# A two-layer hybrid trunk on one core: elementwise chains moved into PSUM, and the mixer's norms, scan outcome and projection order rewritten

## The chip, the core and the metric

The kernel runs on one core of one Trainium2 chip, as one launch. The metric is device time in microseconds (us), the median of several executions. Beside it stands one execution that the hardware profiler recorded; all rows of the profile and of the trace come from that one.

A core has five engines with queues of their own, each of which works through its instructions in a fixed order: PE multiplies matrices (its weight loads, PEld, are shown apart), DVE, ACT and POOL work on elements, and SP issues DMAs. PE writes its results into PSUM, of which the kernel uses eight banks of 128 x 512 fp32. The other data lie in SBUF.

## The reference

Input is x, 512 positions of width 1024, in fp32. Sixteen learned meta tokens are put ahead, so the trunk runs over 528 positions. DEPTH is 2:

```
layer 0:  h += even_mixer(h);              h += mlp(h)
layer 1:  h += conformer_conv_module(h);   h += mlp(h)

even_mixer: u = rms_norm(h); q, k, v, z, xBC, dt = u @ w_in
    q, k: RMS norm per head (8 query heads, 2 key heads, 64 wide)
    att = attention over a window of 128 plus the meta tokens, with ALiBi and sinks
    xBC = silu(causal conv of 4 taps)
    y = state-space scan in chunks of 128 (16 heads, 2 groups, state of 64) + x * d_skip
    y = rms_norm per group of (y * silu(z))
    out = concat(att, y) @ w_out                    (1536 -> 1024)
conformer: u = rms_norm(h) @ pw1 (1024 -> 2048) + b; u = u[:1024] * sigmoid(u[1024:])
    u = causal depthwise conv, 31 taps; u = silu(layer_norm(u)); out = u @ pw2 + b
mlp: square(relu(rms_norm(h) @ w_up)) @ w_down      (1024 -> 4096 -> 1024)
```

The sixteen meta positions are dropped from the output.

## The kernel before

**Layout and precision.** Activations lie with the 1024 features as eight tiles of 128 partitions and the positions along the columns. The positions are cut into two streams: A (stream 0) has 272 columns, the 16 meta tokens and 256 positions, or 256 where the meta tokens are no longer needed; B (stream 1) has 256. Every dense product is made from two halves of each operand: a high part rounded to the matmul's fp32r type and a low part, the rest. A product of weights w and inputs x is hi(w)·hi(x) + hi(w)·lo(x) + lo(w)·hi(x), so each tile of 128 x 128 weights costs three matmuls. In the names, wh and wl are the parts of the weights, xh and xl, nh and nl, ah and al, oh and ol those of inputs. An output tile of 128 features with 8 input tiles takes 24 matmuls; eight such tiles, one half (up or down) of a quarter of the MLP for one stream, take 192.

**Weights.** SP loads them in pieces of 128x512 (pool wm) and, from out-projection 1 on, also 128x1024 (wp). ACT makes the high part (wh), and DVE or POOL the low part (wl = wr − wh).

**Who sets the order.** The program is written as generators ("threads": the main stream of products, the loader, the splitters, one for each tile's eviction, one for each norm and so on) that yield single operations with an estimated duration. A list scheduler (class Sched, lines 66 to 227) takes in each step, among the threads' next operations, the one that it believes can start first, by priority where starts are equal, and emits it to its engine; where an operation may go to DVE or to POOL it takes the one that it believes ends first. A number added to one of these ways is the `bias` for wl: with 0 the two are equal, with 3000 POOL is preferred. So each engine's order is fixed before the program runs, and it is the order of the scheduler's beliefs. All operations are recorded at the lines of the small helpers: L253 (two tensors, DVE) and L255 (POOL), L260 (scalar and two tensors, DVE), L267 (tensor and scalars, DVE), L275 (activation, ACT), L279 (copy or cast, ACT), L282 (copy, DVE), L288 (DMA), L307 (matmul), L314 (transpose on PE), L520 (reciprocal, DVE). For this reason the rows are told apart by the names of tiles.

**PSUM.** The eight banks are three of the kind "mm" (outputs of the dense products), three "bg" (norms, the scan, statistics) and two "at" (attention, convolution sums). Function pmm takes an "mm" bank and may borrow up to `wide` banks of "bg"; wide is 2 from out-projection 1 on.

**The stages** (function main), with the MLP's names: up, the layer, the quarter, the stream.

1. In-projection, 24 tiles for both streams (names in), in the order B, C, k, v, four of q, eight of x, eight of z (W_B to W_Z). Beside it run the threads of the norm, dt, the convolution of 4 taps, q/k norm (th_qk_norm), attention (att_a scores, att_b transposes of probabilities, att_c values), the scan (ssd_a to ssd_h) and its gated norm (ssd_norm: sn_a, sn_b).
2. Out-projection of stream A (out), which starts when the gated norm of A (norm0) is done, then two quarters of the MLP of A (up00A, dn00A, up01A, dn01A), beside which the mixer of B ends; out-projection of B; the other two quarters of A.
3. pw1 of A (pw), then the whole MLP 0 of B (up00B to dn03B); beside it DVE makes the depthwise convolution of A (th_conv, 31 taps of 256 columns for each of eight tiles, summed in two "at" banks; names conv, and Y for the last tap) and its layer norm (th_ln: names lna, lnm, ln, stln).
4. pw1 of B and pw2 of A (both pw), then the MLP 1 of A (up10A to dn13A), with the convolution and the layer norm of B beside it.
5. pw2 of B and the MLP 1 of B (up10B to dn13B), at whose end the outputs are stored.

**The chains that evict a tile.** For an up tile (ev_up in mlp): ut (SBUF) = max(psum, 0) · rb on DVE, and the bank is dropped; uq = square(ut) on ACT; ah = round(uq) on ACT; al = uq − ah on DVE or POOL. rb is the row norm's factor, spread over the partitions, so the norm is applied behind the product. For a tile that becomes the next norm's input (out-projection, the last dn quarter, pw2): h = psum + h on DVE, the bank is dropped, and then function prep makes nh = h · g (ACT), nl = h · g − nh (DVE), the square sqh (ACT) and acc += sqh (DVE) from h in SBUF. When all eight are there, row_norm sums acc over the partitions with a matmul by ones (st...), makes 1/sqrt by a root (ACT), a reciprocal and a Newton step of small DVE operations (rs_v, rs_t, rs_r), spreads it with a second matmul and copies it to rb (ACT). For pw1 (ev in pw1): ut = psum · rb, the bank is dropped; sg = sigmoid(ut + b) for one of two tiles, U = (ut + b) · sg for the other. The layer norm adds eight Y tiles on DVE (lna), takes their mean by a matmul, copies it to lnm, centres Y, squares and adds (lna), spreads the factor to rb, multiplies (Y), and makes silu and the two parts from SBUF.

Of the kernel before, what the change touches and what calls it, by code (L numbers as in the profile page):

```python
# [65 lines left out]
class Sched:  # L66
# [110 lines left out]
    def step(self):  # L177
# [27 lines left out]
        for th in self.threads:  # L205
# [5 lines left out]
            if op.table and op.table != self.table and op.ways[0][0] == "A":  # L211
                t += 1283
            p = th[1]
            key = (t, p() if callable(p) else p, th[4])
# [15 lines left out]
def trunk(ctx: ExitStack, tc: tile.TileContext, h0, vecs, cmat, selm, selmt, atab, atab0, w_in, w_dt, w_out,  # L230
# [127 lines left out]
    cm = const.tile([128, 520], F32, name="cm")  # L358
    ident, mle, mgt, ones = cm[:, 0:128], cm[:, 128:256], cm[:, 256:384], cm[:, 384:512]
    heads = cm[:, 512:520]  # L360
# [11 lines left out]
    bias = [0.0]  # L372
# [144 lines left out]
    def rsqrt(r, t, v):  # L517

        yield ACT(t, v, AF.Sqrt)
        yield VEC(1.04 * cols(r) + 150, lambda: nc.vector.reciprocal(r, t), r, t)  # L520
# [8 lines left out]
    def row_norm(s, a, blocks, eps, key):  # L529
# [6 lines left out]
                   for i, c in enumerate(blocks)))  # L536
# [8 lines left out]
                    ident[0:blk(c)[1], 0:blk(c)[1]], True, True) for i, c in enumerate(blocks)))  # L545
        yield CP(rb[s][:, :n], p[:, :n])
# [20 lines left out]
    def sumsq(a, x, first, begun, pool=False):  # L567
# [5 lines left out]
        else:  # L573
            q = yield take(tmp, [128, 272], F32, "sqh", 3)
# [3 lines left out]
            drop(q)  # L578
# [167 lines left out]
    conv4 = set()  # L746

    def th_silu():
# [9 lines left out]
        for s in range(2):  # L758
            yield lambda: conv4 >= set(range(W_Z, W_Z + 8))
            for k in range(0, 8, 4):  # L760
                x = sz[s][:, k:k + 4, :STREAM[s][1]]
                yield ACT(x, x, AF.Silu)
            done.add(f"z{s}")
# [28 lines left out]
    selr = m1.tile([10, 5, 128], F32R, name="selr")  # L792
    seltr = m1.tile([128, 5, 10], F32R, name="seltr")

    def th_qk_norm():

        yield after("sel")
        p = []
        for s in range(2):
            p.append((yield bank("bg", "qk_a")))  # L800
        for i in range(5):
            yield lambda: (W_K if i == 0 else W_Q + i - 1) in conv4
            x = kf if i == 0 else qf[:, i - 1]
# [41 lines left out]
        drop(a, b)  # L845
# [795 lines left out]
```

## Time and profile before

| | us |
| --- | --- |
| median of 3 runs | 1308.71 (1303.02 to 1311.38) |
| the profiled execution's own time | 1308.62 |
| its span, from first to last instruction | 1306.5 |
| PE busy in the span | 1241.0 (95%) |
| DVE busy | 960.0 (73%) |
| ACT busy | 679.4 (52%) |
| POOL busy | 487.8 (37%) |

The mean clock that was granted to PE is 0.969 of full speed. 2.1 us of the execution lie outside the span.

How to read the views: the windows give, for stretches of the span, each engine's busy microseconds with the number of instructions, and then the clock granted to PE, the busy share of the DMA engines and GB/s. A row of the groups gives line, engine, operation, out<-in with shapes, the count, busy microseconds, the mean nanoseconds of one, and the idle time ahead of them with what ended it. A row of the waits gives which instruction waited for which, the sum, how often and the longest. The chain is read back from the last instruction to what released it; a row has the start, the length and what ran. An fp32 matmul (not fp32r) is recorded as two instructions.

### The profile page before, as it was taken

Reading aid. Unit: us, or ns where it says so; the run is one execution under the profiler, and the core shown is the slowest. Engines: PE = TensorE matmul, PEld = TensorE weight load, DVE = VectorE, ACT = ScalarE, POOL = GpSimd, SP = SyncE. Lnnn points to the kernel's source line nnn. Section 1 sums busy time; section 2 is a strip of 40 time slices with the busy share of each in tenths; the row PEclk is TensorE's granted clock in tenths of the full one; section 3 lists DMA queues with packets and bytes.
Section 4 is the critical chain, followed back from the end, with each engine's and each line's share of the span. In section 5 each row is a group of like instructions: output and inputs, shape, how many; then the busy total and the mean of one; then the engine's idle time right before and its main releaser. Section 6 shows DMA issues by size and latency. Waiting matters only on the chain.

```text
span 1306.5 us, 25401 instructions
## 1 busy us (share of the span) xinstructions
PE 1241.0 (95%) x9798; PEld 1198.1 (92%) x9798; DVE 960.0 (73%) x1928; ACT 679.4 (52%) x1235; POOL 487.8 (37%) x302
## 2 busy tenths in 40 slices
PE   7999998999999999999999988787899889999999
PEld 6998885799999999999999988787899889999998
DVE  6678667787877756589999775898998565756664
ACT  7654445565565645545545555443455364645542
POOL 0000122201110000398888876764798774100000
PEclk9999997899999999999999989888999898999999
DMA  5332110154456655465654444552555446566653
GB/s 180 99 96 72 58 57 26 46 167 121 146 165 222 221 184 167 138 200 176 195 185 155 152 155 133 158 161 82 161 180 181 142 129 205 189 190 191 186 180 103
DMA packets 80060, 194.42 MB, mean 149 GB/s; under 512 B 9090, under 2 KB 16580, under 8 KB 79940
## 3 DMA queue, kind: packets, MB, share of 16 engines
q1 hardware_dynamic: 79940, 192.80, 47.7%
q8 instruction: 77, 1.26, 0.4%
q14 instruction: 43, 0.35, 0.1%
HBM read 190.67 MB, written 2.10 MB: 148 GB/s over the span
## 4 chain that ended last, share of the span: by engine, by line
PE 80%; DVE 16%; issue 2%; ACT 1%; DMA 0%; SPq 0%; DVEq 0%; ACTq 0%
PE in L307 10%; PE pw L307 9%; DVE conv L260 7%; PE out L307 5%; DVE al L253 2%; PE up00A L307 2%; PE dn00A L307 2%; PE up02A L307 2%; PE dn01A L307 2%; PE dn02A L307 2%; PE up03A L307 2%; PE up01A L307 2%; PE dn03A L307 2%; PE up10B L307 2%; PE up13A L307 2%; PE up13B L307 2%
## 5 line engine op out<-in xcount | busy, mean ns | idle before, releaser
L279 ACT CAST wh<-wr 128x512 fp32r<-128x512 f32 (+1 forms) x494 | 382.5, 800 | 288.8 <-PE pw L307 26.9
L255 POOL TENSOR_TENSOR wl<-wr,wh 128x1024 fp32r<-128x1024 f32 (+1 forms) x214 | 421.3, 1991 | 258.1 <-ACT wh L279 237.1
L253 DVE TENSOR_TENSOR wl<-wr,wh 128x512 fp32r<-128x512 f32 x280 | 238.4, 862 | 80.4 <-ACT wh L279 77.2
L260 DVE SCALAR_TENSOR_TENSOR conv<-U,vec,conv 128x256 f32<-128x256 f32 x464 | 208.6, 485 | 6.5
L307 PE MATMUL in<-xh,wh 128*128 128x272 f32 (+1 forms) x384 | 103.4, 296 | 7.2 <-ACT wh L279 6.8
L275 ACT ACTIVATE uq<-ut 128x256 f32<-128x256 f32 (+1 forms) x128 | 53.3, 420 | 98.0 <-DVE ut L260 83.5
L307 PE MATMUL in<-xl,wh 128*128 128x272 f32 (+1 forms) x384 | 100.7, 288 | 0.6 <-DVE xl L260 0.5
L255 POOL TENSOR_TENSOR al<-uq,ah 128x256 fp32r<-128x256 f32 (+1 forms) x24 | 21.0, 876 | 190.9 <-ACT ah L279 190.9
L307 PE MATMUL pw<-nl,wh 128*128 128x256 f32 (+1 forms) x320 | 83.8, 294 | 4.1 <-DVE nl L253 3.8
L307 PE MATMUL pw<-nh,wh 128*128 128x256 f32 (+1 forms) x320 | 83.3, 292 | 3.8 <-DVE ut L253 2.2
L253 DVE TENSOR_TENSOR al<-uq,ah 128x256 fp32r<-128x256 f32 (+1 forms) x88 | 69.2, 792 | 20.7 <-ACT ah L279 20.7
L307 PEld LDWEIGHTS in<-xh,wh 128*128 128x128 f32 x384 | 73.0, 190 | 11.2 <-ACT wh L279 6.8
L307 PEld LDWEIGHTS in<-xl,wh 128*128 128x128 f32 x384 | 72.8, 190 | 2.0 <-DVE xl L260 1.6
L307 PEld LDWEIGHTS pw<-nl,wh 128*128 128x128 f32 x320 | 62.5, 195 | 5.5 <-DVE nl L253 4.6
L307 PE MATMUL in<-xh,wl 128*128 128x272 f32 (+1 forms) x384 | 67.1, 291 | 0.2 <-DVE wl L253 0.2
L307 PEld LDWEIGHTS pw<-nh,wh 128*128 128x128 f32 x320 | 62.4, 195 | 4.3 <-issue 2.4
L307 PEld LDWEIGHTS in<-xh,wl 128*128 128x128 f32 x384 | 54.6, 190 | 3.8 <-issue 2.3
L275 ACT ACTIVATE nh<-h,vec 128x256 fp32r<-128x256 f32 (+1 forms) x48 | 24.4, 513 | 51.4 <-DVE h L253 26.1
L307 PE MATMUL pw<-nh,wl 128*128 128x256 f32 (+1 forms) x320 | 49.5, 288 | 0.0
L279 ACT CAST ah<-uq 128x256 fp32r<-128x256 f32 (+1 forms) x112 | 44.9, 407 | 2.7
L307 PEld LDWEIGHTS pw<-nh,wl 128*128 128x128 f32 x320 | 43.8, 193 | 0.0
L715 POOL MEMSET pad<- 128x3 f32 x10 | 1.2, 118 | 105.0 <-ACT at L279 55.7
(529 smaller groups left out, 3725.8 us busy)
## 6 DMA issues: line engine op xcount, KB each, us to landing
wr<-in_w_up SPq DMA_DIRECT2D x84, 512.0 KB, 3.6
wr<-in_w_dn SPq DMA_DIRECT2D x84, 512.0 KB, 4.0
wr<-in_w_up SPq DMA_DIRECT2D x88, 256.0 KB, 4.3
wr<-in_w_dn SPq DMA_DIRECT2D x88, 256.0 KB, 4.1
wr<-in_w_p SPq DMA_DIRECT2D x36, 512.0 KB, 3.6
wr<-in_w_in SPq DMA_DIRECT2D x48, 256.0 KB, 2.9
wr<-in_w_out SPq DMA_DIRECT2D x36, 256.0 KB, 2.9
wr<-in_w_p SPq DMA_DIRECT2D x24, 256.0 KB, 4.6
```

The lines of the kernel that those rows point to most:

```text
L253: ways = [("V", 1.04 * n + 145, lambda: nc.vector.tensor_tensor(o, a, b, op=op), sb(a) and sb(b))]
L255: ways.append(("G", 2.17 * n + 170, lambda: nc.gpsimd.tensor_tensor(o, a, b, op=op), True))
L260: lambda: nc.vector.scalar_tensor_tensor(o, a, s, b, op0=op0, op1=op1), sb(a) and sb(b))],
L275: return Op([("A", ns, lambda: nc.scalar.activation(o, a, f, **kw), False)], aps(o, accum), aps(a, scale, bias), table=TABLE.get(f, 0))
L279: return Op([("A", 0.836 * cols(o) + 192, lambda: nc.scalar.copy(o, a), False)], [o], [a])
L307: nc.tensor.matmul(o, lhsT=l, rhs=r, start=st, stop=sp)
L715: yield Op([("G", 200, lambda: nc.gpsimd.memset(pad[:, 0:3], 0.0), True)], [pad[:, 0:3]], [])
```

## The change

It is made in many places of one file. No product of weights is added or removed.

- **MLP up.** Relu and factor, square, and al now work on the PSUM bank in place; ah is a copy from it; al is on DVE only, and the bank is dropped at the end. The tiles ut and uq are not used for it.
- **Norm inputs (prep).** The sum with h is made in place in PSUM; nh, nl and the square read PSUM, the square lies in the bank's other half, and ACT copies the sum to h (48 more copies); the bank is dropped at the end.
- **pw1.** The product with rb is made in place, sigmoid and U read the bank.
- **Layer norm.** The mean is made by eight fp32 matmuls a stream (a constant matrix of 1/1024 by Y) that add up in a bank; centring and the row factor read PSUM; squares and silu results lie in halves of banks; no part of it goes to POOL. Its threads' priority goes from 2 to 1.
- **q/k norm.** Sums over a head's 64 features are made by 25 small fp32 matmuls of two columns, with positions on the partitions (128 x 50 in the place of 10 x 528), and spread back with 64-column matmuls. The selection matrices selm and selmt with their loads go; the constant matrix cm grows from 520 to 650 columns.
- **Scan outcome.** The exponential is made in place in PSUM and multiplied from there by DVE (wt); the outcome is made transposed at once (xdt stationary, wt moving, ssd_e), and the part from the state is transposed into the same bank. The transposes ssd_h, the addition to y and its copies go.
- **In-projection.** The order becomes B, C, half of x, k, v, q, the other half of x, z; silu(z) is made by quarters, and the gated norm no longer waits for the whole in-projection before its gate.
- **Out-projection of A.** It begins with three tiles' first four input tiles (attention's, 36 matmuls) before norm0.
- **Scheduler.** The penalty of a change of ACT's table counts only for threads of low priority; the estimate for a reciprocal grows; wide is 1 instead of 2; the bias for wl is 600 instead of 0 at the start; att(3) waits also for att(2) and ssd(2).

The instructions of the two programs by engine, before and after: PE 9550 and 9591, DVE 1930 and 1866, ACT 1205 and 1248 (with two more table loads), POOL 307 and 333, SP 556 and 550. Of the 128x512 pieces of wl DVE makes 126 in the place of 196 and POOL 158 in the place of 88; the 128x1024 pieces stay, 84 and 126.

The core of the diff:

```diff
@@ mlp, ev_up
-            t = yield take(lt[0], [128, 272], F32, "ut", 2)
-            yield STT(t[:, :w], p[:, :w], 0.0, rb[s][:, :w], ALU.max, ALU.mult)
+            u = p[:, :w]
+            yield STT(u, u, 0.0, rb[s][:, :w], ALU.max, ALU.mult)
+            yield ACT(u, u, AF.Square)
+            yield CP(ah[:, j, :w], u)
+            yield TT(al[:, j, :w], u, ah[:, j, :w].bitcast(F32), ALU.subtract)
             drop(p)
-            u = yield take(lt[0], [128, 272], F32, "uq", UQ)
-            yield ACT(u[:, :w], t[:, :w], AF.Square)
-            drop(t)
-            yield CP(ah[:, j, :w], u[:, :w])
-            o = TT(al[:, j, :w], u[:, :w], ah[:, j, :w].bitcast(F32), ALU.subtract, True)
...
@@ prep
-            yield ACT(x, hk, AF.Copy, scale=gk)
-            yield STT(y, hk, gk, x.bitcast(F32), ALU.mult, ALU.subtract)
+            hp = p[:, :n]
+            yield other(hp)
+            yield ACT(x, hp, AF.Copy, scale=gk)
+            yield STT(y, hp, gk, x.bitcast(F32), ALU.mult, ALU.subtract)
             cnt.add(k)
-            yield from sumsq(acc[s][:, xo:xo + n], hk, k == 0, begun)
+            yield CP(hk, hp)
+            yield from sumsq(acc[s][:, xo:xo + n], hp, k == 0, begun, False, p[:, 256:512] if n == 256 else None)
+            drop(p)
...
@@ th_ln
-            yield TT(a, yk(0), yk(1), ALU.add)
-            for k in range(2, 8):
+            p = yield bank("bg", "ln")
+            for k in range(8):
                 yield after(f"conv{s}{k // 4 * 4}")
-                yield TT(a, a, yk(k), ALU.add)
-            p = yield bank("bg", "ln")
-            yield BM((p[:, :n], ones, a, True, True))
+                yield BM((p[:, :n], mean, yk(k), k == 0, k == 7))
...
@@ ssd, outcome
-                yield ACT(wq, pv, AF.Exp)
+                yield ACT(pv, pv, AF.Exp)
+                yield TT(wt[q4][:w, :, :w], pv, cbm[:w, g, :w].unsqueeze(1).to_broadcast([w, 4, w]), ALU.mult)
                 drop(q)
-                yield TT(wq, wq, cbm[:w, g, :w].unsqueeze(1).to_broadcast([w, 4, w]), ALU.mult, True)
...
+    ORDER = [0, 1, *range(W_X, W_X + 4), *range(2, 8), *range(W_X + 4, W_X + 8), *range(16, 24)]
...
-        yield from out_proj(0, pr(0))
+        yield from out_proj(0, pr, 3)
...
-        wide[0] = 2
+        wide[0] = 1
```

What this does to the engines' order is not in the diff, since the scheduler makes it. Three places follow; helper lines are one higher after the change.

On PE, the end of the in-projection. Before, from the last decays and the late attention of A (kc and qf are keys and queries, sn_a and sn_b the gated norm's sums and spread factors) to the first product of out:

```order
L307 MATMUL att_c_2826<-pmt_2822,vspread 128x128 x4
L307 MATMUL att_a_2911<-kc_2883,qf 128x272
L307 MATMUL att_a_2912<-kc_2883,qf 128x272
L307 MATMUL sn_a_2914<-cm,sqa_2853 128x1 x3
L307 MATMUL sn_a_2914<-cm,sqa_2854 128x1 x3
...
L307 MATMUL sn_b_2972<-cm,rs_rsn_2931 128x16
L307 MATMUL sn_b_2972<-cm,rs_rsn_2931 128x128 x2
L307 MATMUL out_3002<-oh,wh_2497 128x272
```

After, from the last products of the in-projection:

```order
L308 MATMUL in_2616<-xh_90,wl_2413 128x256 x4
L308 MATMUL ssd_d_2655<-R_2638,mgtr 128x512
L308 MATMUL ssd_d_2655<-R_2641,mgtr 128x512
L308 MATMUL ssd_e_2677<-cm,y_2610 128x128 x4
L308 MATMUL ssd_e_2677<-wt_2629,xdt_2498 64x128 x4
L308 MATMUL ssd_e_2677<-wt_2631,xdt_2498 64x128 x4
L308 MATMUL out_2713<-oh,wh_2528 128x272
L308 MATMUL out_2713<-ol,wh_2528 128x272
...
L308 MATMUL sn_b_2903<-cm,rs_rsn_2862 128x128 x2
L308 MATMUL out_2713<-xh_89,wh_2665 128x272
```

Between the last product of the in-projection and the first of out that needs the gated norm, 81 instructions stood on PE before, all of attention, scan and gated norm; now 50 of these kinds stand there, with 36 products of out among them.

On DVE, the statistics of the layer norm of A (rs_vln to rs_rln). Before, where the last dn half of B is evicted:

```order
L267 TENSOR_SCALAR rs_vln_9844<-stln_9823 128x2
L253 TENSOR_TENSOR al_5687<-uq_9814,ah_5686 128x256
L520 RECIPROCAL rs_rln_9849<-rs_tln_9850 128x2
L253 TENSOR_TENSOR h<-dn03B_9787,h 128x256
L253 TENSOR_TENSOR h<-dn03B_9825,h 128x256
L260 SCALAR_TENSOR_TENSOR nl_5160<-h,vec,nh_5159 128x256
L253 TENSOR_TENSOR h<-dn03B_9876,h 128x256
L260 SCALAR_TENSOR_TENSOR nl_5160<-h,vec,nh_5159 128x256
L253 TENSOR_TENSOR rs_tln_9850<-rs_rln_9849 128x2
```

After:

```order
L268 TENSOR_SCALAR rs_vln_9294<-stln_9278 128x2
L254 TENSOR_TENSOR h<-dn02B_9273,h 128x256
L521 RECIPROCAL rs_rln_9300<-rs_tln_9301 128x2
L254 TENSOR_TENSOR rs_tln_9301<-rs_rln_9300 128x2
L254 TENSOR_TENSOR rs_tln_9301<-rs_tln_9301,rs_vln_9294 128x2
L268 TENSOR_SCALAR rs_tln_9301<-rs_tln_9301 128x2
L254 TENSOR_TENSOR h<-dn02B_9313,h 128x256
L254 TENSOR_TENSOR rs_rln_9300<-rs_rln_9300,rs_tln_9301 128x2
L261 SCALAR_TENSOR_TENSOR Y<-Y,vec,stln_9369 128x256 x3
L261 SCALAR_TENSOR_TENSOR up03B_9349<-up03B_9349,rb_82 128x256
L254 TENSOR_TENSOR nl_2920<-stln_9369,nh_2919 128x256
```

They moved ahead by a half of the MLP, stand together, and the split that follows (Y, nl) lies between the evictions of up03B; before, it followed in the next pw1.

On DVE, the statistics of the norm ahead of up10A (rs_vfn to rs_rfn), with taps of the convolution of B between them. Before, the last part:

```order
L267 TENSOR_SCALAR rs_tfn_11233<-rs_tfn_11233 128x2
L260 SCALAR_TENSOR_TENSOR conv_10103<-U,vec,conv_10103 128x256
L260 SCALAR_TENSOR_TENSOR conv_10104<-U,vec,conv_10104 128x256 x2
...
L260 SCALAR_TENSOR_TENSOR conv_10104<-U,vec,conv_10104 128x256 x2
L260 SCALAR_TENSOR_TENSOR conv_10103<-U,vec,conv_10103 128x256 x2
L253 TENSOR_TENSOR rs_rfn_11232<-rs_rfn_11232,rs_tfn_11233 128x2
```

After:

```order
L254 TENSOR_TENSOR rs_tfn_11020<-rs_tfn_11020,rs_vfn_11009 128x2
L261 SCALAR_TENSOR_TENSOR conv_9982<-U,vec,conv_9982 128x256
L268 TENSOR_SCALAR rs_tfn_11020<-rs_tfn_11020 128x2
L261 SCALAR_TENSOR_TENSOR conv_9983<-U,vec,conv_9983 128x256
L254 TENSOR_TENSOR rs_rfn_11019<-rs_rfn_11019,rs_tfn_11020 128x2
```

Between the last two steps of the chain stood 21 taps, and now one; over the whole chain 28 and now eight.

More of the change, by code (lines that the diff above doesn't have):

```diff
@@ L371, in trunk @@
     split = [0]
-    bias = [0.0]
+    bias = [600.0]
     turn = deque(["wm"])
@@ L573, in sumsq @@
         else:
-            q = yield take(tmp, [128, 272], F32, "sqh", 3)
+            q = at if at is not None else (yield take(tmp, [128, 272], F32, "sqh", 3))
             yield ACT(q[:, :n], x, AF.Square)
@@ L1352, in main @@
             spawn(ev_in(n, (p, q)), 1, "inev")
-        for n in range(2, 24):
+        for n in ORDER[2:]:
             b, pcs = [], []
@@ L1482, in th_ln, with places, place @@
-            mu = lp.tile([128, 256], F32, tag="lnm", bufs=1, name=nm("lnm"))
-            yield ACT(mu, p[:, :n], AF.Copy, scale=1.0 / D)
-            drop(p, a)
-            a = yield take(lp, [128, 256], F32, "lna", 2)
+                yield BM((p[:, :n], mean, yk(k), k == 0, k == 7))
+            halves = []
+            def places(p, *at):
+                halves[:] = [p[:, i:i + n] for i in at]
+            def place():
+                return lambda: [halves.pop()] if halves else None
+            q = yield bank("bg", "lnq")
@@ L1486, in th_ln @@
+            places(q, 0, n)
+            halves.append(p[:, n:2 * n])
+            a = yield take(lp, [128, 256], F32, "lna", 1)
             begun = []
             def centred(k):
-                yield TT(yk(k), yk(k), mu, ALU.subtract, True)
-                yield from sumsq(a, yk(k), k == 0, begun, True)
-            yield from par([centred(k) for k in range(8)], 2, "ln_")
-            yield from row_norm(s, a, blocks, 1e-5, f"ln{s}")
+                yield TT(yk(k), yk(k), p[:, :n], ALU.subtract)
+                if k:
+                    u, = yield place()
+                    yield from sumsq(a, yk(k), False, begun, False, u)
+                    halves.append(u)
+                else:
+                    yield from sumsq(a, yk(k), True, begun)
@@ L1493, in th_ln @@
+            yield from par([centred(k) for k in range(8)], 1, "ln_")
+            drop(p, q)
+            r = yield from row_norm(s, a, blocks, 1e-5, f"ln{s}", True)
             drop(a)
             yield guard
+            q = yield bank("bg", "lnq")
+            places(q, 0, n)
+            halves.append(r[:, n:2 * n])
             def split_(k):
-                y = yk(k)
-                yield STT(y, y, V("lng", k), rb[s][:, :n], ALU.mult, ALU.mult)
-                yield ACT(y, y, AF.Silu, bias=V("lnb", k))
@@ L1500, in split_ @@
-                yield CP(dh[:, k, :n], y)
-                yield TT(dl[:, k, :n], y, dh[:, k, :n].bitcast(F32), ALU.subtract, True)
+                u, = yield place()
+                yield STT(yk(k), yk(k), V("lng", k), r[:, :n], ALU.mult, ALU.mult)
+                yield ACT(u, yk(k), AF.Silu, bias=V("lnb", k))
+                yield CP(dh[:, k, :n], u)
+                yield TT(dl[:, k, :n], u, dh[:, k, :n].bitcast(F32), ALU.subtract)
+                halves.append(u)
                 cnts.setdefault(f"ln{s}", set()).add(k)
-            yield from par([split_(k) for k in range(8)], 2, "ln_")
+            yield from par([split_(k) for k in range(8)], 1, "ln_")
```

233 lines of the change are left out of this document (104 added, 129 removed).

## The prediction, on record before the change was run

> **What bounds the kernel now.** I read the table of stages first, from the windows of the trace; its columns are busy microseconds and instruction counts of PE, PEld, DVE, ACT and POOL, then granted clock, DMA share and GB/s.
>
> ```profile
> 0.00:208.00 208.00, 200.10 (x1539) 178.54 (x1539) 142.78 (x374) 106.51 (x232) 13.20 (x30) 1.00 0.29 88
> 208.00:244.00 36.00, 29.11 (x129) 19.70 (x128) 26.96 (x80) 23.56 (x54) 7.34 (x8) 0.74 0.08 23
> 244.00:405.00 161.00, 161.00 (x1250) 154.81 (x1250) 128.63 (x263) 100.02 (x205) 25.65 (x25) 0.99 0.49 149
> 539.00:587.00 48.00, 47.88 (x381) 47.48 (x380) 31.67 (x64) 20.74 (x29) 37.76 (x20) 1.00 0.52 165
> 587.00:784.00 197.00, 187.51 (x1543) 186.44 (x1542) 175.12 (x333) 99.02 (x167) 164.21 (x89) 0.97 0.54 169
> 784.00:872.00 88.00, 76.41 (x588) 74.35 (x588) 67.53 (x134) 45.81 (x74) 62.93 (x34) 0.90 0.48 149
> 872.00:941.00 69.00, 53.37 (x394) 52.45 (x393) 61.80 (x140) 26.90 (x48) 40.63 (x24) 0.88 0.40 123
> 941.00:1120.00 179.00, 168.22 (x1355) 167.14 (x1354) 125.08 (x220) 92.97 (x160) 124.98 (x69) 0.95 0.54 169
> 1120.00:1306.00 186.00, 183.37 (x1549) 183.17 (x1548) 111.30 (x177) 90.26 (x146) 7.11 (x6) 1.00 0.56 173
> ```
>
> PE is the bound almost everywhere, so a stage is worth changing only by what it stands above PE's floor. The floor is in the chain of waits of the last stage, where one half (192 matmuls of 256 columns, 8 output tiles) takes
>
> ```profile
> 1189.68 22.73 PE dn11B L307 x192
> ```
>
> That is 0.118 us a matmul and 2.84 us a tile. Against it: **F**, 587 to 784, the eight halves up00B to dn03B, has 197 − 8 × 22.73 = 15.2 us of loss. **G**, 784 to 941, is 576 projection matmuls (68.2) and two halves (45.5): 157 − 113.7 = 43.3. **H**, 941 to 1120, is six halves and 192 pw2 matmuls: 179 − 159.1 = 19.9. The mixer's tail, 208 to 244, has PE at clock 0.74 and hardly any projection matmul in it. The last stage has no loss, nor has the stretch from 405 to 539.
>
> The second reading is who keeps PE waiting (waits of PE, 587 to 784 first, then 781 to 1121):
>
> ```profile
> PE dn03B L307 <- DVE al L253: 5.3, 1, 5.3
> PE dn02B L307 <- DVE al L253: 2.7, 1, 2.7
> ...
> PE stfn L307 <- DVE rs_rfn L253: 6.3, 1, 6.3
> PE up10A L307 <- DVE nl L260: 4.9, 1, 4.9
> PE dn12A L307 <- DVE al L253: 3.9, 1, 3.9
> PE pw L307 <- DVE nl L253: 3.8, 3, 1.8
> ```
>
> All end on DVE, which is 89% busy in F. The 201 taps of the row below, 90.5 us, come in the first three quarters and make it fuller there. And much of what DVE does there is slow. Groups of DVE, the last stage first, where POOL is idle (7 of 186 us), then 587 to 781, where it is 83% busy, then 781 to 877:
>
> ```profile
> L253 DVE TENSOR_TENSOR al<-uq,ah 128x256 fp32r<-128x256 f32 x26 | 11.6, 451 | 11.4 <-ACT ah L279 11.4
> L260 DVE SCALAR_TENSOR_TENSOR ut<-up10B,rb 128x256 f32<-128x256 f32 x8 | 3.4, 420 | 5.1 <-PE up10B L307 5.1
> ...
> L260 DVE SCALAR_TENSOR_TENSOR conv<-U,vec,conv 128x256 f32<-128x256 f32 x201 | 90.5, 485 | 2.8
> L253 DVE TENSOR_TENSOR al<-uq,ah 128x256 fp32r<-128x256 f32 x24 | 25.8, 1084 | 0.9 <-ACT ah L279 0.9
> L253 DVE TENSOR_TENSOR lna<-lna,Y 128x256 f32<-128x256 f32 x6 | 10.5, 1743 | 0.0
> L253 DVE TENSOR_TENSOR lna<-lna,sqh 128x256 f32<-128x256 f32 x7 | 7.1, 1015 | 0.1
> L260 DVE SCALAR_TENSOR_TENSOR nl<-h,vec,nh 128x256 fp32r<-128x256 f32 x3 | 5.7, 1888 | 0.9 <-ACT nh L275 0.9
> ...
> L260 DVE SCALAR_TENSOR_TENSOR U<-ut,vec,sg 128x256 f32<-128x256 f32 x8 | 9.5, 1217 | 0.0
> L260 DVE SCALAR_TENSOR_TENSOR nl<-h,vec,nh 128x256 fp32r<-128x256 f32 x7 | 7.6, 1103 | 0.0
> L253 DVE TENSOR_TENSOR acc<-acc,sqh 128x256 f32<-128x256 f32 x6 | 5.6, 934 | 0.3
> ```
>
> The same subtraction takes 451 ns beside an idle POOL and 1084 beside a busy one. Taps, which read one operand in PSUM and one in SBUF, take 485 in the same window. So the trace divides DVE's operations by where the operands lie: two from SBUF pay 0.5 to 1.3 us for POOL's company, one from PSUM pays nothing.
>
> **The change, part by part.**
>
> *Contention.* The MLP chain, the norm inputs, the pw1 eviction and the layer norm now leave a DVE operand in PSUM. In F that takes away 24 × 0.63 (al) + 6 × 1.3 + 7 × 0.57 (lna) + 3 × 1.4 (nl) = 31 us of DVE, of 175. On the other side DVE takes what POOL did and the change takes from it (lines of POOL, whole run):
>
> ```profile
> L255 POOL TENSOR_TENSOR al<-uq,ah 128x256 fp32r<-128x256 f32 x22 | 19.3, 878 | 179.8 <-ACT ah L279 179.8
> L255 POOL TENSOR_TENSOR wl<-wr,wh 128x1024 fp32r<-128x1024 f32 x126 | 304.9, 2429 | 190.5 <-ACT wh L279 185.2 <-PE up03B L307 2.6 <-PE up10A L307 2.2
> L255 POOL TENSOR_TENSOR wl<-wr,wh 128x512 fp32r<-128x512 f32 x88 | 118.3, 1364 | 67.6 <-ACT wh L279 51.9 <-PE in L307 15.7
> ```
>
> about 22 subtractions, 10 us, spread over F, G and H. No subtraction of the MLP can go to POOL any more; in DVE's queue it waits for ACT's ah, with taps and the next evictions behind it, as 88 of them did before. ACT gets 48 copies of h at about 0.42 each (its square of the same size, below), 20 us over stages where it is half busy: it lies beside PE's work. If ACT were full, it would delay the copies that follow, 0.42 a tile.
>
> [...]
>
> *F.* Of 15.2 us, 9.6 are waits (the two rows and two small ones), the rest is the clock, 0.97, that falls behind them. After it DVE's first three quarters hold 201/3 × 0.45 = 30 us of taps and 24 evictions, sums and subtractions at 0.42 to 0.45 = 10, with ends of taps some 42 of 45.5, so I leave 2 us of loss. The layer-norm mean becomes eight matmuls a stream in place of seven DVE additions and one matmul. Their price stands in this row, with two of them (two records each) in 1.2 us:
>
> ```profile
> L307 PE MATMUL ln<-lna,cm 128*128 128x256 f32 x4 | 1.2, 382 | 0.0
> ```
>
> [...] They stand in PE's queue ahead of the MLP's products, so a late tap would stop PE; that is in the low end. Half of 8.4 belongs to F: 15.2 − 2 − 4.2 = **9** (3 if the in-order DVE gives back half, 12 if the matmuls cost the least).
>
> *G.* The rows above and the smaller waits of this stage make up to 29 us; the clocks 0.90 and 0.88 over 157 us make 17. Taken away: U, nl and acc at 781 to 877 fall by 8 × 0.73 + 7 × 0.62 + 6 × 0.5 = 13 us of DVE, and stream 0's layer-norm split (nl from Y) goes from pw1 into up03B, where DVE has room. The statistics' chain in up10A stays but shortens:
>
> ```profile
> 885.10 0.35 PE stfn L307 x4
> ...
> 898.60 1.22 DVE rs_rfn L253
> ...
> 899.95 1.21 PE stfn L307 x4
> ```
>
> Between these rows DVE does 28 taps; in the new order eight stand between the first and the last row of the chain. That is 20 × 0.45 = 9 us less; PE stood 6.3 + 4.9 us and lost clock. I leave 17 of 43.3: the remaining statistics (5), the refilling of the clock (5) and DVE still over 90% (7). Gain **26** (15 if only the stall of stfn and the waits on nl go; 35 if only the statistics remain).
>
> *H.* dn12A and dn13A wait for al. 19.9 less 6 left and 4.2 of matmuls: **10** (4 to 15).
>
> *The mixer's tail.* From the last in-projection matmul on the chain to the first one of out:
>
> ```profile
> 206.29 1.27 PE in L307 x9
> ...
> 209.52 4.01 ACT sz L275 x4
> ...
> 216.31 3.64 PE ssd_e L307 x16
> ...
> 237.11 1.43 PE sn_a L307 x12
> ...
> 244.79 2.62 PE out L307 x16
> ```
>
> 244.79 − 207.56 = 37.2 us, of which the attention of blocks whose q and k came late is the middle. With q, k, v before half of x and all of z, 31 of the 81 side instructions here go into the in-projection, where PE is full: they cost their floor there, about 8 us. Left is: table and silu, 1.3 + 1 (a quarter of the row's 4.01), the last decays and ssd_e (5 to 7), gate and squares (2.7), sn_a (1.4), root and its short chain (4), sn_b and split (2.5), and 36 lead matmuls (4.5, useful work). About 22: 37.2 − 22 + 4.5 − 8 = **11**. Zero if DVE and POOL arrive late with wt and xc; 18 if the moved work fills holes of PE that the first window has (8 us not busy).
>
> [...] I take **0**, −5 to +2. The bias of 600 in the place of 0 hands DVE's wl in the mixer to POOL: 40 pieces, 1.36 us of POOL each, with room there (13 of 208 us busy). Six small loads leave SP's queue and the constants' load grows by a quarter; the in-projection's weights come in the new order, same bytes: nothing, since the DMA share is 0.29 there. If a tile's weights came late, it would cost its own wait once.
>
> Sum: 11 + 0 + 9 + 26 + 10 = 56. The profiled execution took 1308.62 (2.1 outside its span of 1306.5), the median is 1308.71: **1252 us**. All low ends together give 17, or 1292; all high ones 82, or 1227.
>
> **Rivals.** *R1, DVE stays the bound of the conformer.* For: 42 of a quarter's 45.5 us leave it 8%, and it works strictly in order, so a tenth lost in waits for ACT between taps makes it 46.2 and more. Against: PE's waits end on al and nl, which get shorter. Then F gives nothing (9 less) and G only the 15 of its low end: 1272. *R2, the contention moves to the mixer.* POOL's 40 more wl there make two-SBUF operations slow, wt and xl above all; then the tail's 11 goes and 8 come on top: 1271. Against: POOL would still be under half busy. *R3, other side: banks.* The chain in place holds a PSUM bank longer, and one bank fewer may be borrowed. The hold is
>
> ```profile
> L275 ACT ACTIVATE uq<-ut 128x256 f32<-128x256 f32 x32 | 13.2, 417 | 22.9 <-DVE ut L260 22.5 <-POOL al L255 0.2 <-DVE al L253 0.2
> L279 ACT CAST ah<-uq 128x256 fp32r<-128x256 f32 x32 | 12.8, 405 | 0.8
> ```
>
> 0.42 + 0.42 + 0.41 + 0.45 = 1.7 us, plus queueing, against 0.42 before. With three banks a tile costs (2.84 + hold)/3, so it decides from a hold of 5.7 us (with the fourth borrowed, from 8.5). At 9 it costs 3.95, 1.1 us over the floor, and on the 64 tiles of the eight up halves of F, G and H that is 71 us: the gain of 56 turns into a loss of 15, 1324. For: DVE runs in order behind taps. Against: it takes queueing of more than four times the work, with a bank to borrow in most places.
>
> **How the numbers follow.** The forecast has 0.58, R1 0.18, R2 0.14, R3 0.10. Range 1226 to 1290, from the ends above (1227, 1292): it holds the forecast, R1 and R2 but for their far ends, and leaves out R3. A measurement of this kernel tells about 1% from no change, 1295.6 below: faster 0.82, same 0.09 (R1 and R2 together, or a mild R3), slower 0.09 (R3).
>
> **What would show it.** al, nl, acc and U near 0.45 in all windows; stages of F at 23 us a half; up10A under 32 us instead of 41; the tail under 25 us. Wrong: waits of PE for a bank with ah or al as releaser (R3), wl or wt over 1 us on DVE before 245 us (R2), F still near 195 with taps in the chain (R1).

## The result, and the profile after

The changed kernel takes 1260.76 us (median of 4 runs, 1258.36 to 1261.81) against 1308.69 us (4 runs, 1303.02 to 1311.38) before: a ratio of 0.9637, 95% interval 0.9602 to 0.9671. The forecast was 1252. The profiled execution's span fell from 1306.5 to 1256.6 us, and the mean granted clock of PE rose from 0.969 to 0.990.

The windows of the changed kernel, cut where its stages begin (columns as in the prediction):

```profile
0.00:211.00 211.00, 203.10 (x1636) 181.90 (x1637) 127.82 (x327) 109.08 (x231) 44.47 (x55) 1.00 0.30 87
211.00:239.00 28.00, 22.01 (x140) 17.66 (x139) 20.66 (x57) 15.27 (x27) 8.67 (x8) 0.81 0.20 58
239.00:406.00 167.00, 166.96 (x1279) 155.07 (x1278) 116.67 (x264) 107.67 (x239) 57.04 (x44) 0.98 0.46 139
...
591.00:778.00 187.00, 186.29 (x1564) 185.68 (x1563) 147.30 (x354) 106.81 (x193) 155.18 (x81) 1.00 0.58 181
778.00:848.00 70.00, 68.69 (x583) 68.48 (x582) 49.05 (x120) 39.18 (x65) 57.38 (x31) 1.00 0.58 178
848.00:903.00 55.00, 50.70 (x404) 50.28 (x403) 48.40 (x123) 25.06 (x45) 39.10 (x21) 0.94 0.49 157
903.00:1065.00 162.00, 161.09 (x1358) 160.67 (x1357) 97.97 (x231) 91.04 (x163) 116.72 (x61) 1.00 0.62 189
1065.00:1256.00 191.00, 183.79 (x1553) 183.18 (x1551) 113.31 (x184) 89.11 (x149) 0.00 (x0) 1.00 0.54 167
```

F (now 591 to 778) has 147 us of DVE in place of 175 and a full clock; pw1 of B with pw2 of A takes 70 us in place of 88. The last stage is longer: 191 us in place of 186.

Groups of DVE in F, the same as in the prediction's fence:

```profile
L254 DVE TENSOR_TENSOR al<-up00B,ah 128x256 fp32r<-128x256 f32 x8 | 3.3, 419 | 0.3 <-ACT ah L280 0.2
L261 DVE SCALAR_TENSOR_TENSOR nl<-dn03B,vec,nh 128x256 fp32r<-128x256 f32 x7 | 3.3, 482 | 3.1 <-ACT nh L276 3.1
L254 DVE TENSOR_TENSOR Y<-Y,ln 128x256 f32<-128x256 f32 x8 | 2.8, 414 | 2.6 <-PE ln L308 2.2 <-ACT ln L276 0.5
L254 DVE TENSOR_TENSOR lna<-lna,lnq 128x256 f32<-128x256 f32 x4 | 1.7, 420 | 0.4 <-ACT lnq L276 0.3
```

With one operand in PSUM all of them take 0.41 to 0.48 us beside a POOL that is still 83% busy (155 of 187 us). The five longest of PE's waits behind 410 us:

```profile
PE up10A L308 <- DVE al L254: 4.3, 1, 4.3
PE up10B L308 <- DVE al L254: 2.9, 1, 2.9
PE pw L308 <- ACT sg L276: 2.5, 2, 1.3
PE up02A L308 <- DVE acc L254: 1.9, 1, 1.9
PE up10B L308 <- DVE acc L254: 1.6, 1, 1.6
```

They are of a new kind. An up matmul does not read the low part al that its own chain makes, nor acc: these two are the last readers of a bank, so the wait is read as one for a bank that the next tile wants.

The stages by the first matmul of each, in the profiled execution of each kernel (us; the runs are told of below). "Start" runs from the first matmul, 6 to 7 us into the span, to the first product of out, "tail" from there to up00A, "A" from up00A to out-projection 1, F, G and H as in the prediction, "last" from up10B to the last matmul, 3.3 us before the end of the span:

| run | start | tail | A | out1 to pw1 | pw1 of A | F | pw of G | up10A, dn10A | H | last |
| --- | --- | --- | --- | --- | --- | --- | --- | --- | --- | --- |
| before | 237.7 | 50.3 | 110.8 | 131.2 | 50.2 | 197.1 | 88.2 | 69.0 | 179.1 | 182.8 |
| after | 207.6 | 69.4 | 122.3 | 133.9 | 51.3 | 186.7 | 70.4 | 54.8 | 162.5 | 187.3 |
| tab_alone | 238.3 | 51.3 | 110.8 | 131.2 | 51.1 | 187.9 | 89.7 | 68.6 | 177.5 | 182.8 |
| tab_old | 206.6 | 69.3 | 126.1 | 135.4 | 55.5 | 189.6 | 75.6 | 54.1 | 162.5 | 187.3 |
| conf_only | 237.9 | 47.6 | 114.0 | 131.8 | 56.8 | 190.0 | 76.2 | 55.0 | 162.8 | 187.7 |
| mixer_only | 207.6 | 66.4 | 124.6 | 131.2 | 51.1 | 187.5 | 90.9 | 68.4 | 175.5 | 182.2 |
| mlp_old | 207.6 | 69.0 | 122.3 | 135.5 | 51.3 | 192.8 | 70.7 | 53.1 | 163.6 | 186.2 |
| prep_old | 207.6 | 67.0 | 130.4 | 131.9 | 51.7 | 186.8 | 78.3 | 60.7 | 161.6 | 187.0 |
| ln_old | 208.0 | 68.4 | 122.3 | 135.3 | 51.3 | 188.1 | 74.2 | 51.9 | 167.4 | 190.3 |
| pw1_old | 207.6 | 69.7 | 122.3 | 133.9 | 50.8 | 186.9 | 70.4 | 55.4 | 162.7 | 187.4 |
| wide2 | 207.6 | 69.6 | 122.3 | 133.9 | 51.3 | 186.7 | 70.4 | 52.1 | 162.5 | 184.4 |
| qk_old | 217.2 | 58.2 | 126.4 | 134.0 | 51.3 | 187.1 | 70.6 | 54.9 | 162.8 | 187.9 |
| hybrid | 207.6 | 68.6 | 122.3 | 131.7 | 51.3 | 186.9 | 70.7 | 55.1 | 161.2 | 182.2 |
| combined | 207.6 | 69.1 | 122.3 | 131.7 | 50.8 | 187.1 | 69.4 | 49.6 | 161.6 | 182.2 |

The first three columns belong together, since the start of out-projection A moved ahead of the gate. Before, out-projection 1 begins at 405.5 us, after at 406.2. So the whole gain comes behind the mixer: 10.4 in F, 32.0 in G, 16.6 in H, less 8.3 in three places that the prediction had at nothing (2.7, 1.1 and 4.5). Each row is one execution. That of the changed kernel (1258.36 us) is the fastest of its four and that of mlp_old (1263.84) the slowest, so a difference of rows need not be that of the medians.

### The profile page after: what moved, and what is told of

Its sections match the earlier page's. It is cut to its first block, busy times and chain, and to the rows that moved or that the text cites. A ratio compares the mean times of both kernels' runs of the same rounds, so it can differ in the third digit from the quotient of the medians.

```text
span 1256.6 us, 25583 instructions
## 1 busy us (share of the span) xinstructions
PE 1224.3 (97%) x9960; PEld 1183.7 (94%) x9960; DVE 842.1 (67%) x1864; ACT 680.2 (54%) x1278; POOL 536.5 (43%) x328
## 3 DMA queue, kind: packets, MB, share of 16 engines
q8 instruction: 78, 1.28, 0.4%
## 4 chain that ended last, share of the span: by engine, by line
PE 92%; DVE 3%; ACT 3%; issue 1%; POOL 0%; DMA 0%; SPq 0%; DVEq 0%; ACTq 0%
PE in L308 12%; PE pw L308 9%; PE out L308 5%; PE up00A L308 2%; PE dn00A L308 2%; PE up01A L308 2%; PE dn01A L308 2%; PE dn02A L308 2%; PE up03A L308 2%; PE up10A L308 2%; PE up12A L308 2%; PE dn13B L308 2%; PE dn12B L308 2%; PE dn03B L308 2%; PE dn00B L308 2%; PE dn11B L308 2%
## 5 line engine op out<-in xcount | busy, mean ns | idle before, releaser
L256 POOL TENSOR_TENSOR wl<-wr,wh 128x512 fp32r<-128x512 f32 x284 | 507.6, 1805 | 427.0 <-ACT wh L280 354.5
L254 DVE TENSOR_TENSOR wl<-wr,wh 128x512 fp32r<-128x512 f32 (+1 forms) x210 | 197.8, 954 | 97.4 <-ACT wh L280 91.7
L308 PE MATMUL pw<-nh,wh 128*128 128x256 f32 (+1 forms) x320 | 80.3, 284 | 2.5 <-ACT sg L276 2.5
L308 PE MATMUL pw<-nl,wh 128*128 128x256 f32 (+1 forms) x320 | 80.0, 284 | 0.0
L308 PEld LDWEIGHTS in<-xh,wl 128*128 128x128 f32 x384 | 55.4, 191 | 4.4 <-issue 3.2
L308 PE MATMUL out<-xh,wh 128*128 128x272 f32 (+1 forms) x128 | 34.4, 297 | 0.0
L308 PE MATMUL out<-xl,wh 128*128 128x272 f32 (+1 forms) x128 | 34.1, 295 | 0.0
L254 DVE TENSOR_TENSOR pw<-pw,rb 128x272 f32<-128x272 f32 (+1 forms) x32 | 14.1, 441 | 26.0 <-PE pw L308 26.0
L308 PEld LDWEIGHTS out<-xh,wh 128*128 128x128 f32 x128 | 25.2, 197 | 0.4 <-issue 0.4
L308 PEld LDWEIGHTS out<-xl,wh 128*128 128x128 f32 x128 | 25.2, 197 | 0.4 <-POOL xl L256 0.4
```

Source lines behind the costliest of these rows:

```text
L254: ways = [("V", 1.04 * n + 145, lambda: nc.vector.tensor_tensor(o, a, b, op=op), sb(a) and sb(b))]
L256: ways.append(("G", 2.17 * n + 170, lambda: nc.gpsimd.tensor_tensor(o, a, b, op=op), True))
L308: nc.tensor.matmul(o, lhsT=l, rhs=r, start=st, stop=sp)
```

## The experiments

Theory C, formed from this table: the contention that the prediction describes made the gain in the conformer, and the mixer's edits made none. First the two halves were taken apart, and two of the chains in place undone.

**The mixer undone (conf_only).** The scheduler's lines, the order of the in-projection, q/k norm, scan outcome and the lead of the out-projection go back; for instance

```diff
-        expect([w_in[n] for n in ORDER], 8)
-        expect([w_out[n] for n in range(8)], 12, 3, 4)
+        expect([w_in[n] for n in range(24)], 8)
+        expect([w_out[n] for n in range(8)], 12)
```

> All that the change does in the mixer is undone (order of the in-projection, q/k norm, scan outcome, lead of the out-projection, the scheduler's penalty and the bias of wl); MLP, norm inputs, pw1 and layer norm stay in PSUM. The layer norm's mean uses the matrix of ones and the factor 1/1024 in the centring, for room in SBUF. Theory C (the conformer's part made the whole gain, the mixer's none): 1260 us, between 1256 and 1265, out-projection 1 begins at 405 us +- 2. Rival M (the mixer's tail did bring its 11 us, and something in the other part took as much): 1268 to 1273.

Measured: 1271.36 us (1270.92 to 1272.55; ratio to before 0.9716, 0.9701 to 0.9730), which is M's number. But the place is C's: out-projection 1 begins at 406.1. What is lost against the changed kernel lies in pw1 of A (+5.5), F (+3.3) and G (+6.0), where nothing of the mixer runs. Both theories fell.

**The conformer undone (mixer_only).** ev_up, prep, pw1 and the layer norm go back to SBUF and `wide` to 2.

> The other half alone: the mixer's edits stay, and MLP, norm inputs, pw1 and layer norm go back to tiles in SBUF; two banks may be borrowed again. Theory C: no gain, 1306 to 1311, tail of A shorter by about 10 us and up00A to dn01A longer by about as much. Rival M: 1295 to 1300.

Measured: 1297.67 us (ratio 0.9915, 0.9900 to 0.9930): M's number again, and again not in the mixer: out-projection 1 begins at 405.1. 9.6 of its 11 us are in F.

What the two have in common is neither the mixer nor the conformer but the scheduler, which I had put on the mixer's side. Theory T: it is the line that charges a change of ACT's table only to threads of low priority.

**That line alone (tab_alone), and all but that line (tab_old).** On the kernel before:

```diff
-            if op.table and op.table != self.table and op.ways[0][0] == "A":
-                t += 1283
             p = th[1]
-            key = (t, p() if callable(p) else p, th[4])
+            p = p() if callable(p) else p
+            if op.table and op.table != self.table and p > 1:
+                t += 1283
+            key = (t, p, th[4])
```

> Before, with one line of the change alone: the scheduler adds the price of a change of ACT's table only for threads of low priority. Theory T (this line, not the mixer's edits, made the 11 us of the run with the mixer's part alone): 1296 to 1300, the same stages from 680 us on. Rival (it took the mixer's edits): 1306 to 1311.

Measured: 1300.67 us (ratio 0.9942, 0.9922 to 0.9961), near T's range and clear of the rival; F is 187.9 in place of 197.1.

> After, with this one line undone alone. Theory T: 1269 to 1274 as with the mixer undone, PE waits 8 us in pw for the sigmoid sg, whose bank in place cannot be freed before it, since ACT's table change stands behind casts of weights. Rival N (the bias or the reciprocal's estimate made the difference): 1259 to 1263.

Measured: 1273.95 us (ratio 0.9740, 0.9718 to 0.9762): T. The line is worth 8 us on the kernel before and 13 on the changed one, and in two ways. On the changed one it guards the bank. The chain of waits of tab_old in pw1 of A:

```profile
557.54 2.52 ACT wh L279 x4
560.06 0.02 issue
560.08 1.28 ACT L275
561.36 0.01 issue
561.37 0.50 ACT sg L275
561.87 0.04 issue
561.91 37.68 PE pw L307 x288
```

and its waits:

```profile
PE pw L307 <- ACT sg L275: 8.4, 2, 4.2
```

Four casts of weights (2.52 us) stand ahead of the table load (1.28) and the sigmoid, because the scheduler thought that a change of table is dear; the sigmoid's tile now is the bank itself, so PE stops, twice 4.2 us. Before the change the sigmoid read ut and the bank was long free. In the changed kernel the same wait is 2.5 us, so this explains 5.9 of the 13 us; the rest (A is 3.8 us longer, with a wait of 2.6 us for xl, and F 2.9) was not followed. On the kernel before, the line does something else: in F, PE's waits for al at dn02B and dn03B shrink. The timeline of DVE in the kernel before has, at the end of up03B,

```profile
750.58 3.62 DVE L253 TENSOR_TENSOR al<-uq,ah 128x256 fp32r<-128x256 f32 x2
754.12 5.06 DVE L253 TENSOR_TENSOR lna<-lna,sqh 128x256 f32<-128x256 f32 x2
759.10 0.41 DVE L260 SCALAR_TENSOR_TENSOR ut<-up03B,rb 128x256 f32<-128x256 f32 x1
759.44 1.48 DVE L253 TENSOR_TENSOR al<-uq,ah 128x256 fp32r<-128x256 f32 x2
```

Two additions of the layer norm take 5.06 us beside POOL (busy for all 10 us from 750 to 760) and stand ahead of the last al; with the line, the orders differ, and PE's waits for al in F are 0.9 us in place of 9.2. That the place of these additions makes the difference is not shown: with the line, two al at the same place take 4.33 us together, and PE waits 0.5 us at dn03B. By which steps of the planner the line moves them was not followed.

**MLP chain back to SBUF (mlp_old).**

```diff
-            yield TT(al[:, j, :w], u, ah[:, j, :w].bitcast(F32), ALU.subtract)
-            drop(p)
+            o = TT(al[:, j, :w], u[:, :w], ah[:, j, :w].bitcast(F32), ALU.subtract, True)
```

> After, with the MLP's up eviction alone back to tiles ut and uq in SBUF, al again on DVE or POOL. Contention theory: al back to about 1.08 us on DVE between 590 and 1040 us, 48 of them with 0.65 us more each, 31 us of DVE; F, G and H lose 10 to 25 us together: 1270 to 1285. Rival O (what counted was that the layer norm's split moved ahead and the statistics stand together, not how long al takes): under 1264.

Measured: 1261.19 us (1259.71 to 1263.84; ratio 0.9633, 0.9617 to 0.9649): no difference to the changed kernel, which is the rival's number; the 10 to 25 us of the contention theory did not come. The price per operation came back, the time did not. Groups of DVE, 590 to 1040 us:

```profile
L254 DVE TENSOR_TENSOR al<-uq,ah 128x256 fp32r<-128x256 f32 x46 | 49.9, 1093 | 11.2 <-ACT ah L280 11.2
```

The table says where it went: F loses 6.1, H 1.1 and the stretch to pw1 1.6, and G's up10A wins 5.8 (24.6 in place of 30.4), since its banks are free as soon as ut is written; dn10A gives 4.1 of that back, 3.5 of it in waits for al. So the chain in place is worth 6 us in F and costs about as much where banks are short.

**Norm inputs back to SBUF (prep_old).**

```diff
-            yield ACT(x, hp, AF.Copy, scale=gk)
-            yield STT(y, hp, gk, x.bitcast(F32), ALU.mult, ALU.subtract)
+            yield ACT(x, hk, AF.Copy, scale=gk)
+            yield STT(y, hk, gk, x.bitcast(F32), ALU.mult, ALU.subtract)
```

> After, with the norm inputs alone (out, dn03, pw2) back to h in SBUF before nh, nl and square. Theory P (the longer chain in place, 3.3 us a tile between ACT and DVE against 2.84 us of PE, is what up02A and up10B lost): up02A back to 24 us and up10B to 23.5, 7 us gained, but nl and acc above 0.9 us again from 778 to 848 us, where 4 to 10 us go: 1256 to 1266 in all. Rival (a bank too few): up02A and up10B stay at 27 and 28.

Measured: 1275.98 us (ratio 0.9745, 0.9729 to 0.9760), a loss of 15, more than either said. G loses 13.8, where PE waits 4.8 us for nl at up10A again, and A 8.1, of which dn00A's wait for xl is 2.8 and the rest was not followed. In G's first part the price is that of the prediction:

```profile
L261 DVE SCALAR_TENSOR_TENSOR nl<-h,vec,nh 128x256 fp32r<-128x256 f32 x5 | 8.4, 1689 | 1.3 <-ACT nh L276 1.3
```

up10B does not come back (28.3); up02A does for the most part (25.7).

**Layer norm back to SBUF (ln_old).**

```diff
-                yield BM((p[:, :n], mean, yk(k), k == 0, k == 7))
+                yield TT(a, a, yk(k), ALU.add)
```

> After, with the layer norm alone back in SBUF (sums on DVE, one matmul for the mean, squares and silu in SBUF, parts to DVE or POOL, priority 2). Contention theory: lna and Y at 1.0 to 1.2 us again on some 40 operations, 25 us more of DVE in the quarters where it is full or its chain ends a stage: 1268 to 1282, the loss at dn02B to dn03B and dn11A to dn13A. Rival (the layer norm was hidden): the 14 matmuls less bring 3 to 6 us, 1255 to 1258.

Measured: 1269.61 us (ratio 0.9704, 0.9684 to 0.9724): the contention theory. H loses 4.9, pw of G 3.8, F 1.4; the last stage loses 3.0, up10A with dn10A wins 2.9. The stall in H is at dn13A, where PE waits for DVE's addition ut, the one that frees the bank. Groups of DVE, 590 to 1040 us, and a row of the waits:

```profile
L261 DVE SCALAR_TENSOR_TENSOR Y<-Y,vec,rb 128x256 f32<-128x256 f32 x16 | 18.7, 1208 | 0.0
L254 DVE TENSOR_TENSOR lna<-lna,Y 128x256 f32<-128x256 f32 x12 | 14.1, 1172 | 0.0
L254 DVE TENSOR_TENSOR lna<-lna,sqh 128x256 f32<-128x256 f32 x13 | 13.8, 1063 | 0.7
```

```profile
PE dn13A L308 <- DVE ut L254: 3.5, 1, 3.5
```

**pw1 back to SBUF (pw1_old).**

```diff
-                yield TT(t, t, rb[s][:, :n], ALU.mult)
+                yield TT(t[:, :n], p[:, :n], rb[s][:, :n], ALU.mult)
+                drop(p)
```

> After, with pw1's eviction alone back to a tile in SBUF. Contention theory: U at 1.2 us again, 16 operations, 6 to 10 us of DVE in the stretch where taps fill it: 1263 to 1269. Rival (the bank freed at once is worth as much): waits of PE for sg vanish, 1256 to 1261.

Measured: 1259.77 us (1258.45 to 1261.97): the rival, no difference. U is slow again (1009 ns in the mean of 8) and pw1 of A 0.5 us shorter. That edit cancels out.

**Two banks to borrow (wide2).** `wide[0] = 1` becomes 2.

> After, with two banks of bg to borrow instead of one, as before. Theory B (the chain in place holds a bank until al or acc, and PE waits for the bank at up10A 4.3, up10B 2.9 and 1.6, up02A 1.9 us): these waits fall by half, 1250 to 1256. Rival (the tiles arrive late in any case, the chain of nh, nl, acc and the casts of weights sets the pace): 1258 to 1262.

Measured: 1252.39 us (1252.22 to 1253.03; ratio 0.9570, 0.9551 to 0.9588): theory B. The changed kernel had given away a bank exactly where its chains hold them longer. Waits:

```profile
PE up02A L308 <- DVE acc L254: 1.9, 1, 1.9
PE up10A L308 <- DVE al L254: 1.8, 1, 1.8
PE up10B L308 <- DVE acc L254: 1.6, 1, 1.6
```

up10A's fell from 4.3 to 1.8, up10B's for al is gone; those for acc stay, so there one more bank to borrow was no cure, for a reason that was not followed. Of the 8.4 us between the medians the rows of the table hold 5.6.

**q/k norm undone (qk_old).** Sums and spreading by matmuls of ten rows, selm and selmt loaded again.

> After, with the q/k norm alone as before (sums and spread by matmuls of 10 rows, reciprocal over 10 x 528). The layer norm's mean is made with the matrix of ones and the factor in the centring, for room in SBUF. Theory Q (its new small matmuls cost PE 5.3 us in the mixer, which is where part of the mixer's gain went): out-projection 1 begins at 400 to 402 us instead of 406, 1254 to 1257. Rival (the old norm brings attention late and the time goes there): out-projection 1 at 405 to 408, 1259 to 1265.

Measured: 1257.90 us, but from 1251.31 to 1261.79 and so not told apart from the changed kernel (ratio 0.9606, 0.9570 to 0.9641). Out-projection 1 begins at 408.2: the rival's place. The price Q speaks of is real: groups of PE of the changed kernel, up to 406 us,

```profile
L308 PE MATMUL qk_b<-cm,qkr 128*64 128x128 f32 x80 | 6.3, 284 | 0.0
L308 PE MATMUL qk_a<-cm,sqk 128*128 128x2 f32 x40 | 5.4, 253 | 0.0
```

are 11.7 us, and 14.0 with two small forms, for what took 8.8 in all its forms before. But with the old norm the last products of the attention and of the decays stand behind the in-projection again and lose as much: its last product ends at 205.5 us in place of 212.0, and the first of out begins at 223.5 in place of 214.5.

**SBUF where POOL is idle (hybrid).** In the last stage POOL does nothing (0.00 in the window above), and little in out-projection 1 (5.4 of 34 us) and pw2 of B (0.5 of 24), so chains in PSUM should save little there and hold banks. Norm inputs of out-projection 1 and of pw2 of B, and the tiles of up10B, go back to SBUF:

```diff
+            if (key, s) in (("fn", 1), ("nx", 1)):
+                yield other(hk, hp)
+                drop(p)
...
+            if layer == 1 and q == 0 and s == 1:
+                t = yield take(lt[0], [128, 272], F32, "ut", 2)
```

> After, with the chains of SBUF for the norm inputs of out-projection 1 and pw2 of B and for up10B alone, where POOL is idle or nearly so. Theory B: up10B back from 28.6 to about 23.7 us, up02A from 27.1 to about 25.5, 1253 to 1256. Rival (casts of weights set the pace there): no change, 1258 to 1262.

Measured: 1249.48 us (1248.96 to 1249.79; ratio 0.9546, 0.9531 to 0.9562): theory B's places, and better than its range: up10B takes 23.6 us, as before the change, up02A 25.0 in place of 27.1, and H, which it did not name, wins 1.3. What went wrong there in place is to be seen in the changed kernel's chain of waits, pw2 of B:

```profile
1046.39 0.49 DVE nl L261
...
1049.77 0.41 DVE nl L261
1050.46 0.38 ACT pw L276
1050.84 0.97 ACT wh L280
1051.83 0.45 DVE wl L254
1052.28 0.70 issue
1052.97 0.49 DVE nl L261
```

One nl every 3.3 us against PE's 2.84 us a tile: square, cast of weights (0.97) and wl of DVE take turns between the steps of one tile, each engine waiting for the other, with the bank held through all of it.

**All three (combined).** hybrid, pw1_old and wide2 together.

> The three undoings that did not lose, together: SBUF chains for the norm inputs of out-projection 1 and pw2 of B and for up10B, pw1's eviction in SBUF, and two banks of bg to borrow. Theory B (the losses that are left are waits for banks, each in its own place): 1249.5 less 3 at up10A less 1 to 2 at pw: 1244 to 1247, up10A at 27.7 us, no wait of PE for sg. Rival (the same waits are relieved twice): 1248 to 1251.

Measured: 1243.29 us (5 runs, 1242.93 to 1244.30; ratio 0.9504, 0.9485 to 0.9523), the fastest of all and a little under theory B's range. Of the five waits of the changed kernel one is left, at up10A; no other that remains behind 410 us is over 0.8 us:

```profile
PE up10A L308 <- DVE al L254: 0.8, 1, 0.8
```

## Why the prediction was right, point by point

The sign, the range (1226 to 1290) and the size (48 of the 56 us) came out. The steps did not all, and that the sum came so near is in part luck: against the terms of the sum the mixer fell short by 11.7 us, F, G and H gave 1.4, 6.0 and 6.6 more, and 8.3 were lost where the prediction had nothing; and one line without any price in it made 13 of the 48 us.

*Prices.* Two operands in SBUF beside POOL against one in PSUM: right in the groups shown, 0.9 to 1.9 against 0.41 to 0.48 us, and they come back in each run that undoes a part. In the last stage, with POOL idle, al took 451 ns from SBUF before and takes 417 to 420 from PSUM after.

*F: 9 forecast, 10.4 measured, by another road.* I had let al's price carry the term. The scheduler's line alone, with every chain in SBUF, gives 9.2 of F; all chains in PSUM without the line give 7.5. Either is enough, so they do not add. The line was missing from my working altogether: I had listed it in the change and given it no price, and it is worth 13 us in the changed kernel.

*G: 26 forecast, 32.0 measured.* Undone parts of G: norm inputs 13.8, the line 4.5 and layer norm 0.9 net, pw1 0.6, MLP −1.4 (in place it loses there). The statistics' chain shortened as worked out: up10A went from 41.2 to 30.4 us (under 32, as forecast), and its wait for nl (4.9) and that of stfn (6.3) are gone.

*H: 10 forecast, 16.6 measured.* Layer norm 4.9, MLP 1.1; the rest was not taken apart. The two mean chains, one for each stream, cost 7.6 us of PE for 16 matmuls, 0.475 each, so 14 more cost 6.4 where the prediction had 8.4, 14 times the 0.6 us that its row shows; for a least price, on which the 12 for F rests, it had no run. Only 1.9 falls in H, which was charged 4.2:

```profile
L308 PE MATMUL ln<-Y,cm 128*128 128x256 f32 x32 | 7.6, 379 | 0.0
```

*The mixer: 11 forecast, −0.7 measured.* The failed step is "31 of the 81 side instructions here go into the in-projection". The tail did get shorter, though not under the 25 us that were to show it: from the end of the in-projection's last product to the first product of out that needs the gated norm it takes 27 us (212.0 to 238.8), and up00A starts 10.8 us earlier. But nothing of the attention went into the in-projection. Part of it went the other way, behind the tail. Windows of att_b on PE, before and then after:

```profile
0.00:208.00 208.00, 4.30 (x26) 1.00 0.29 88
208.00:244.00 36.00, 3.50 (x17) 0.74 0.08 23
244.00:294.00 50.00, 1.59 (x10) 0.98 0.48 139
294.00:405.00 111.00, 0.97 (x8) 1.00 0.50 154
```

```profile
0.00:211.00 211.00, 4.09 (x26) 1.00 0.30 87
211.00:239.00 28.00, 0.00 (x0) 0.81 0.20 58
239.00:283.00 44.00, 0.00 (x0) 0.92 0.45 127
283.00:406.00 123.00, 5.32 (x34) 1.00 0.47 143
```

The in-projection holds 26 transposes (att_b) and 28 products with the values (att_c) in both kernels, and of the scores (att_a) 32 in place of 44. All 34 late transposes now run from 283 on, with the 32 late products with values and 16 of the 32 late scores, and A is 11.5 us longer; the other 16 scores stand in the tail, 5.3 us as before. Up to out-projection 1 PE is busy for 390.2 of 405 us before and 392.1 of 406 after: side work that leaves one hole lands on PE elsewhere. The small matmuls of the q/k norm alone take PE 5.2 us more (14.0 in place of 8.8), where the prediction had put the in-projection's side matmuls at 0 in all. No run shows that 0; over the whole run, ssd_e's products of 128 partitions fell from 18.2 to 9.0 us, and its new ones by cm took 8.4 where ssd_h's had taken 5.7. Its sum for the tail had a slip as well: 37.2 − 22 + 4.5 − 8 is 11.7, and the parts listed for "about 22" add up to 22.4 to 24.4. The two kernels without one or the other half, conf_only and mixer_only, end the mixer within 1 us of each other, too. A condition that was in the diff, att(3) waiting for att(2) and ssd(2), fits this; it was not tried alone.

*Rivals.* R1 did not come: F is at 23.3 us a half. R2 neither: wl on DVE in the first 211 us takes 689 ns, as before (686). R3 came in small, with the right mechanism: waits for banks held until al and acc make 10.7 us of those shown above; one bank more makes the median 8.4 us shorter, SBUF chains in the last stage and out-projection 1 11.3. I had put its threshold at 8.5 us of holding and all of it on the up tiles; what I had not costed are the norm inputs, whose chain has six steps, and the lead tiles of up10A and up10B, which wait for the norm's factor with the bank in hand. "It lies beside PE's work", said of the 48 copies, does not hold in up02A and up10B, where they are one of the six steps; how much of the loss is theirs was not taken apart.

## What to carry to other kernels

Moving elementwise chains into PSUM traded DVE time (175 to 147 us in F) for bank time (10.7 us of waits): here it paid where POOL is busy beside a chain that ends a stage (norm inputs 15 us, layer norm 9), paid nothing on balance for the MLP, which won in F and lost as much in waits for banks, nor for pw1, and cost where POOL is idle or nearly so (11.3 us). In a kernel whose order is planned, price each line of the planner like an edit of its own, and undo it alone: here one line was worth more than three of the four rewritten chains. Work that leaves a hole on the bounding engine has to be followed to where it lands before the hole is counted as gain.

## What the runs showed of the hardware

POOL paid little of the contention here. Its low parts of weights take, in the changed kernel, whole run:

```profile
L256 POOL TENSOR_TENSOR wl<-wr,wh 128x1024 fp32r<-128x1024 f32 x126 | 302.1, 2404 | 102.7 <-ACT wh L280 99.1 <-ACT lna L276 2.0 <-PE dn10A L308 1.4
L256 POOL TENSOR_TENSOR wl<-wr,wh 128x512 fp32r<-128x512 f32 x158 | 207.6, 1327 | 324.2 <-ACT wh L280 255.4 <-PE in L308 27.8 <-PE out L308 23.3
```

against 2429 and 1364 before. In F alone, where no DVE operation with two large operands in SBUF is left, they went from 2450 to 2404 ns and from 1355 to 1294, 2 to 5%: nearly all of the loss was DVE's, up to 5.06 us for two additions of the layer norm, where four others in F took 417 ns each. Small operations were slow as well: the statistics of the layer norm stayed in SBUF, and of their six steps on 128x2 elements in F two took 2.1 and 2.2 us, the others 0.15 to 0.17; that POOL is the cause there too is not shown.
